# A decoder trunk with mixture-of-experts layers: expert matmuls in a fixed order, longer runs of expert weights, and one adaLN form for all tiles

## The chip, the cores and the metric

The kernel runs on one core of a Trainium2 chip. The metric is the device time of one launch in microseconds (us). A core has TensorE (PE, matrix multiplies; its loads of the stationary operand are shown apart as PEld), VectorE (DVE), ScalarE (ACT), GpSimd (POOL) and SyncE (SP, which here only issues transfers). Sixteen DMA engines move data between HBM and the core's SBUF; matmuls accumulate in PSUM.

## The reference

Two layers on 512 tokens of width 1024, float32. Each has a token mixer (layer 0: sparse attention; layer 1: HGRN2, a gated linear recurrence) and then a mixture of experts. Every sub-layer has an RMS norm, and an adaLN shift, scale and gate made from one conditioning vector `c`.

```python
cond = silu(c)
for layer in range(2):
    mod = einsum('bd,sde->sbe', cond, ada_w[layer]) + ada_b[layer][:, None, :]   # s: mixer, experts
    shift, scale, gate = split(mod[0], 3, axis=-1)
    h = rms_norm(x, norm_g[layer, 0]) * (1.0 + scale[:, None, :]) + shift[:, None, :]
    y = nsa_mixer(h, ...) if layer == 0 else hgrn2_mixer(h, ...)
    x = x + gate[:, None, :] * y
    shift, scale, gate = split(mod[1], 3, axis=-1)
    h = rms_norm(x, norm_g[layer, 1]) * (1.0 + scale[:, None, :]) + shift[:, None, :]
    # experts: top group of 4, then the top 2 of its 4 experts for each token; 16 experts in all
    #   expert(t) = (silu(t @ w1[e]) * (t @ w3[e])) @ w2[e],  w1, w3: 1024 x 512, w2: 512 x 1024
    y = hier_moe(h, ...)
    x = x + gate[:, None, :] * y
```

`ada_w` is 2 x 2 x 1024 x 3072; the kernel treats it as 24 tiles of 1024 x 512, 6 for each of the four sub-layers.

## The kernel before

The stages follow each other: mixer of layer 0 (to about 420 us), its output product and the routing (to 500), its experts (to 775), mixer of layer 1 (to 1105), its output product and the routing (to 1180), its experts (to 1450), and the last sums. In the trace's names: `w` is a 2 MB tile of any weights, `hg` gathered token rows, `hgt` their transpose, `h_ps` the hidden products, `g` the gated hidden rows, `gT` their transpose, `y_ps` the output products, `yd` the results' rows in HBM, `xnd` the normalised token rows in HBM, `ada_ps` an adaLN product, `Q`, `K`, `Tc` the level operands of the recurrence.

*Experts* (`Moe.experts`). Sixteen positions p, fullest expert first; position p takes at most `CAPS[p]` rows: 96 three times, 128 once, 96 six times, 64 six times. A row block of 64 (or 32) rows is the stationary operand, and 2 (or 4) matmuls that write different column groups of PE run side by side: `BLOCKS` cuts 96 into 64 + 32 and 128 into 64 + 64. For each expert:
- `gather` (L1416, POOL): the rows from `xnd`.
- `transposed` (L1428 on PE; the shift and scale are applied as the transposes leave PSUM, on ACT and DVE).
- `hidden` (L1452): w1 and w3 against the transposed rows, in two halves of the 1024 inputs; then silu on ACT (L1456) and the product with the w3 side on DVE (L1458).
- `hidden_T` (L1465): four transposes of the gated rows, left by ACT as `gT`.
- `store` (L1479): w2; the adaLN gate on DVE (L1482); the rows go to `yd`.

The program's order inside one step i is gather and weights of expert i + 4, `hidden_T` of i, `transposed` of i + 2, `store` of i, `hidden` of i + 1. The framework's scheduler may reorder independent instructions on an engine by its own cost estimates; the four calls on PE are independent enough to be interleaved.

Each expert's weights are three 2 MB tiles: the first halves of w1 and w3 (part 0), the second halves (part 1), and w2 (part 2). Nine buffers hold three experts' tiles, and the next load waits for the one that it replaces. Nearly all loads are issued on SP, in the order part 0, 1, 2 (`load_part`: L1196 for w1 and w3, L1200 for w2). Input row k * 128 + p lies in partition p as block k, so w1 and w3 arrive in runs of 2 KB (one row of 512 float32) and w2 in runs of 4 KB.

*adaLN* (`ada_parts`). Tiles 0 to 15 are made by matmuls (L185): the conditioning column is the stationary operand, four column groups side by side, in four steps of eight matmuls (each float32 matmul is two instructions). Tiles 16 to 23 (the gate of layer 1's mixer, and all six of its experts) are made otherwise: ACT scales the eight row blocks by the conditioning value (L192), POOL adds them up in three additions (L198), and four matmuls with a column of ones finish the sum (L202). These eight tiles are worked on between the steps of layer 1's mixer (`merge(heads(), ada, HADA)` in `hgrn_heads`); they share the ring of two weight buffers with that mixer's own weights.

*Layer 1's mixer* (`hgrn_heads`, `hgrn_levels`). For each of eight heads, nine levels: DVE multiplies Q (L1080) and K (L1081) by running products, PE multiplies them in small blocks (L1043, L1057, L1063, L1068, L1073). In between PE works on the input product (`pr_ps`, L337 to L343), which the program advances beside the heads.

*Before the experts* (`mix_out`, `prepare`, `tokens`). Output product, new x, RMS norm of the token rows (`rms_rows`, L251 to L255), which are stored to `xnd` from ACT; the router's logits come from a separate transpose (L1226 writes them).

## Time and profile before

| | us |
|---|---|
| median of 3 runs (lowest, highest) | 1475.61 (1474.67, 1477.06) |
| the profiled execution | 1478.35 |
| its span, first to last instruction | 1476.5 |

| engine | busy us | share of the span |
|---|---|---|
| PE | 1291.1 | 87% |
| PEld | 767.6 | 52% |
| DVE | 723.1 | 49% |
| ACT | 468.1 | 32% |
| POOL | 225.5 | 15% |

HBM is read for 320.73 MB in all. A row of the profile names line, engine, operation, what is written and read by the kernel's names, and shapes; in rows in order of time the first two numbers are start and length in us, and the bracket holds the idle time of the engine before the instruction and what ended it. "issue" means that nothing the profile shows was waited for. Rows that begin with a:b give for a stretch of the span its length, then the busy time of PE, PEld, DVE, ACT and POOL (with counts), PE's granted clock (1.00 is full speed), the mean busy share of the 16 DMA engines and GB/s; an engine that did nothing there is left out.

### The profile page before, as it was taken

To read this page: it belongs to the slowest core of one execution; us is meant where nothing else is said; L and a number is where in the kernel's file an instruction comes from. 1 tells how busy PE (TensorE), PEld (TensorE's weight loads), DVE (VectorE), ACT (ScalarE), POOL (GpSimd) and SP (SyncE) were. 2 spreads that over 40 slices of the span, in tenths; PEclk is the share of its full clock that TensorE was granted. 3 is DMA by queue.
4 is the path that set the end of the run, shared out by engine and by line. 5 is a ranking of instruction groups with operands and counts; after the bars stand their busy time and mean duration, and the time that the engine had idled before them with its cause. 6 is when DMAs were issued, how large, how long until landed. Compare 5 with 4: busy or idle time off the path is not lost. (4 is left out here: it accounts for less than half of the span.)

```text
span 1476.5 us, 25266 instructions
## 1 busy us (share of the span) xinstructions
PE 1291.1 (87%) x10122; PEld 767.6 (52%) x10123; DVE 723.1 (49%) x1791; ACT 468.1 (32%) x1071; POOL 225.5 (15%) x198
## 2 busy tenths in 40 slices
PE   4998899988989699999983998888979699999983
PEld 3776555765558333333323866566767543333330
DVE  2636886468854722222217476777665641222213
ACT  2523555336533211111115434344533121111110
POOL 1202212222100100000014025222130100000002
PEclk9999999999999799999996999999989799999997
DMA  9702552634564899999986222433338699999995
GB/s 354 206 11 85 176 185 91 252 121 152 192 265 157 282 368 343 376 381 334 384 325 182 86 103 87 157 115 115 115 115 299 235 343 365 360 377 335 367 397 193
DMA packets 168733, 346.42 MB, mean 235 GB/s; under 512 B 17236, under 2 KB 40620, under 8 KB 168605
## 3 DMA queue, kind: packets, MB, share of 16 engines
q1 hardware_dynamic: 135984, 276.80, 52.6%
q0 software_dynamic: 10560, 38.54, 8.0%
q10 hardware_dynamic: 22060, 29.34, 6.0%
q8 instruction: 84, 1.38, 0.4%
q14 instruction: 45, 0.36, 0.1%
HBM read 320.73 MB, written 23.93 MB: 233 GB/s over the span
## 5 line engine op out<-in xcount | busy, mean ns | idle before, releaser
L1452 PE MATMUL h_ps<-w,hgt 128*32 128x256 f32 (+1 forms) x2240 | 332.9, 488 | 0.0
L1452 PEld LDWEIGHTS h_ps<-w,hgt 128*32 128x32 f32 (+1 forms) x2240 | 111.8, 123 | 203.1 <-issue 172.4
L1479 PE MATMUL y_ps<-w,gT 128*32 128x256 f32 (+1 forms) x1120 | 163.6, 499 | 2.5 <-ACT gT L1468 2.1
L1458 DVE TENSOR_TENSOR g<-h_ps,g 32x256 f32<-32x256 f32 (+1 forms) x70 | 38.9, 556 | 253.7 <-ACT g L1456 253.1
L1456 ACT ACTIVATE g<-h_ps 64x512 f32<-64x512 f32 (+1 forms) x52 | 26.8, 516 | 368.2 <-PE h_ps L1452 346.2
L337 PE MATMUL pr_ps<-whi,hThi 128*128 128x512 f32 x288 | 119.6, 417 | 1.8 <-DVE qn L498 1.8
L338 PE MATMUL pr_ps<-wlo,hThi 128*128 128x512 f32 x288 | 115.6, 401 | 0.3 <-DVE wlo L311 0.3
L339 PE MATMUL pr_ps<-whi,hTlo 128*128 128x512 f32 x288 | 115.7, 402 | 0.2 <-DVE hTlo L283 0.2
L1479 PEld LDWEIGHTS y_ps<-w,gT 128*32 128x32 f32 (+1 forms) x1120 | 54.9, 125 | 97.3 <-issue 81.3
L1482 DVE TENSOR_TENSOR y<-y_ps,gate 128x512 f32<-128x512 f32 (+1 forms) x52 | 31.1, 598 | 123.3 <-PE y_ps L1479 107.5
L311 DVE TENSOR_TENSOR wlo<-w,whi 128x512 fp32r<-128x512 f32 x120 | 79.7, 702 | 23.0 <-ACT whi L310 22.8
L310 ACT ACTIVATE whi<-w 128x512 fp32r<-128x512 f32 x120 | 70.8, 629 | 39.0 <-SPq L1589 14.2
L782 ACT ACTIVATE P<-P,nm 128x128 f32<-128x128 f32 (+3 forms) x128 | 70.9, 556 | 36.9 <-DVE nm L780 35.8
L1416 POOL DMA_INDIRECT hg<-xnd,gidxp x26 | 23.7, 913 | 384.8 <-PE hg_tp L1428 383.0
L776 PE MATMUL s_ps<-kT,qT 128*128 128x256 f32 (+3 forms) x256 | 64.8, 358 | 12.0 <-DVE qn L498 6.9
L198 POOL TENSOR_TENSOR w<-w 128x2048 f32<-128x2048 f32 (+2 forms) x24 | 67.0, 2792 | 47.3 <-ACT w L192 46.1
L780 DVE CUSTOM_DVE_ANT_0 P<-s_ps,tb 128x128 f32<-128x128 f32 (+3 forms) x128 | 59.5, 485 | 21.5 <-PE s_ps L776 18.8
L1436 DVE TENSOR_SCALAR hgt<-hg_tp,mod 128x96 f32<-128x96 f32 (+2 forms) x128 | 43.7, 365 | 41.9 <-PE hg_tp L1428 36.4
L337 PEld LDWEIGHTS pr_ps<-whi,hThi 128*128 128x128 f32 x288 | 55.6, 193 | 15.1 <-issue 3.3
L339 PEld LDWEIGHTS pr_ps<-whi,hTlo 128*128 128x128 f32 x288 | 55.4, 192 | 12.2 <-DVE hTlo L283 0.4
L338 PEld LDWEIGHTS pr_ps<-wlo,hThi 128*128 128x128 f32 x288 | 55.9, 194 | 11.0 <-DVE wlo L311 0.7
L821 PE MATMUL p_tp<-ident,P 128*128 128x128 f32 x320 | 52.8, 282 | 8.2 <-DVE P L796 7.9
(361 smaller groups left out, 2121.9 us busy)
## 6 DMA issues: line engine op xcount, KB each, us to landing
w<-in_moe_w_dram SPq DMA_DIRECT2D x120, 1024.0 KB, 9.7
w<-in_moe_w_dram SPq DMA_DIRECT2D x32, 2048.0 KB, 9.5
w<-in_ada_w_dram SPq DMA_DIRECT2D x22, 2048.0 KB, 9.3
w<-in_hgrn_w_in_dram SPq DMA_DIRECT2D x12, 1024.0 KB, 6.9
tb<-tabd ACTq DMA_DIRECT2D x16, 456.0 KB, 3.8
yd<-y ACTq DMA_DIRECT2D x56, 128.0 KB, 5.0
w<-in_nsa_w_in_dram SPq DMA_DIRECT2D x3, 2048.0 KB, 8.1
yd<-zero POOLq DMA_DIRECT2D x12, 512.0 KB, 9.6
```

The lines of the kernel that those rows point to most:

```text
L198: nc.gpsimd.tensor_tensor(w[:, 0:n], w[:, 0:n], w[:, n:2 * n], op=ALU.add)
L310: nc.scalar.activation(a, w[:, k], AF.Copy)
L311: nc.vector.tensor_sub(b, w[:, k], a.bitcast(F32))
L337: nc.tensor.matmul(ps, hi[:, k, c], a, start=(k == 0), stop=False)
L338: nc.tensor.matmul(ps, hi[:, k, c], b, start=False, stop=False)
L339: nc.tensor.matmul(ps, lo[:, k, c], a, start=False, stop=(k == NK - 1))
L776: nc.tensor.matmul(sp[:, :n], qT[:, (hd + j) % 8, 128 * t:128 * t + 128], kT[:, v, br, gl, :n], start=(v == 0), stop=(v == 1))
L780: nc.vector.tensor_tensor_reduce(ps, sp[:, :n], tbs[hd + j][:, 384 - 128 * t:512], scale=-1.0, scalar=3.0e38, op0=ALU.add, op1=ALU.min, ac ...
L782: nc.scalar.activation(ps, ps, AF.Exp, bias=nm[:, i:i + 1], scale=-1.0, accum_out=z[:, i:i + 1])
L821: nc.tensor.transpose(tp[:, 128 * (t - kc):128 * (t - kc) + 128], Ps[j][:, offs[t] + 128 * kc:offs[t] + 128 * kc + 128], ident)
L1452: nc.tensor.matmul(ps[m * j:m * j + m, :w], hgt[:, k, r:r + m], ws[half][:, x + i, c:c + w], start=(k == 0), stop=(k == NK - 1))
L1479: nc.tensor.matmul(ps[m * j:m * j + m, :w], gT[:, f, r:r + m], w2v[:, f, w * j:w * j + w], start=(f == 0), stop=(f == 3))
```

## The change

- *Experts' order.* Every PE instruction of the experts gets an ordering edge to the one before it (`pe`), so that PE runs them in the program's order. `hidden` becomes a generator, and one step's order is: half 0 of the first row block of expert i + 1; transposes of the gated rows of i; transposes of the gathered rows of i + 2; half 0 of the second block (or half 1, where there is one block); `store` of i, second block first; half 1 of i + 1; then the gating.
- *Expert weights.* Partition p takes input rows 4 p to 4 p + 3 of a half (of w2: rows 4 p to 4 p + 3), which are one run of 8 KB (16 KB) in HBM. The token rows' columns are permuted to match, in two strided instructions as they are normalised (`spread`); the shift and scale columns are permuted by 16 small matmuls a layer (`modp`, in `prepare`); the gated rows are written to a new tile `go` with a stride.
- *adaLN.* All 24 tiles are made by matmuls; ACT's scaling and POOL's additions of tiles 16 to 23 go.

```diff
         def part(t, w):
-            if 6 * (2 * l + s) + t < POOLED:
-                ps = mm_ps("ada_ps")
...
-            else:
-                for k in range(NK):
-                    nc.scalar.activation(w[:, k], w[:, k], AF.Copy, scale=cond[:, k:k + 1])
...
-                    nc.gpsimd.tensor_tensor(w[:, 0:n], w[:, 0:n], w[:, n:2 * n], op=ALU.add)
...
+            ps = mm_ps("ada_ps")
+            for q in range(0, NK, 2):
+                side_by_side([lambda k=k, g=g: nc.tensor.matmul(
+                    ps[32 * g:32 * g + 32, 0:128], cond[:, k:k + 1].to_broadcast([128, 32]),
+                    w[:, k, 128 * g:128 * g + 128], start=(k == 0), stop=(k == NK - 1))
+                    for k in (q, q + 1) for g in range(4)])
                 yield
...
+    def spread(a):
+        return a.rearrange("q (h p i) -> q h i p", h=2, i=4)
...
-        nc.vector.tensor_scalar(dst, src, rs, None, op0=ALU.mult)
+        if order:
+            for half in range(2):
+                nc.vector.tensor_scalar(dst.rearrange("q (h i p) -> q h i p", h=2, i=4)[:, half], order(src)[:, half],
+                                        rs, None, op0=ALU.mult)
+        else:
+            nc.vector.tensor_scalar(dst, src, rs, None, op0=ALU.mult)
...
+            pp = tp_ps("mp_ps")
+            for i in range(4):
+                for g in range(4):
+                    nc.tensor.matmul(pp[32 * g:32 * g + 32, 4 * i:4 * i + 4], ident[:, i::4], self.mod[:, g::4],
+                                     start=True, stop=True)
+            self.modp = self.pool.tile([128, 16], F32, name="modp")
...
-                    eng.dma_start(out=w[:, 4 * i:4 * i + 4],
+                    eng.dma_start(out=w[:, 4 * i:4 * i + 4].rearrange("p k n -> p (k n)"),
                                   in_=I[name][self.l, e, 512 * part:512 * part + 512]
-                                  .rearrange("o (k p) n -> p (o k) n", p=128))
+                                  .rearrange("o (p k) n -> p (o k n)", p=128))
             else:
...
-                              in_=I["moe_w2"][self.l, e].rearrange("o (f p) n -> p (o f) n", p=128))
+                              in_=I["moe_w2"][self.l, e].rearrange("o (p f) n -> p (o f n)", p=128))
...
+        def pe(self, ins):
+            if self.in_order:
+                if self.last is not None:
+                    edge(ins, self.last)
+                self.last = ins
...
+            n = len(blocks)
+            product(0, 0)
+            yield
+            for b in range(1, n):
+                product(0, b)
+            if n == 1:
+                product(1, 0)
+            yield
+            if n > 1:
+                for b in range(n):
+                    product(1, b)
...
-                    nc.vector.tensor_mul(gt[r:r + m, w * j:w * j + w], ps[64 + m * j:64 + m * j + m, :w],
-                                         gt[r + m * j:r + m * j + m, :w])
-            return gt
+                    nc.vector.tensor_mul(go[r:r + m].rearrange("q (f p) -> q p f", f=4)[:, 2 * m * j:2 * m * j + 2 * m],
+                                         ps[64 + m * j:64 + m * j + m, :w].rearrange("q (p f) -> q p f", f=4),
+                                         gt[r + m * j:r + m * j + m, :w].rearrange("q (p f) -> q p f", f=4))
+            yield go
...
-            for r, m in blocks:
+            for r, m in reversed(blocks):
...
             def steps(i):
                 step("hg", i + 4, lambda p: self.gather(self.slot_tokens(p), CAPS[p]))
                 step("w", i + 4, self.weights)
+                step("h", i + 1, lambda p: self.hidden(S.pop(("hgt", p)), S["w", p], BLOCKS[CAPS[p]]))
+                h = S.pop(("h", i + 1), None)
+                if h:
+                    next(h)
                 step("gT", i, lambda p: self.hidden_T(S.pop(("g", p)), CAPS[p]))
                 step("hgt", i + 2, lambda p: self.transposed(S.pop(("hg", p)), CAPS[p]))
+                if h:
+                    next(h)
                 step("y", i, lambda p: self.store(S.pop(("gT", p)), S.pop(("w", p))[2],
...
-                step("g", i + 1, lambda p: self.hidden(S.pop(("hgt", p)), S["w", p], BLOCKS[CAPS[p]]))
+                if h:
+                    S["g", i + 1] = next(h)
```

More of the change, by code (lines that the diff above doesn't have):

```diff
@@ L181, in part @@
         def part(t, w):
-            if 6 * (2 * l + s) + t < POOLED:
-                ps = mm_ps("ada_ps")
-                for q in range(0, NK, 2):
-                    side_by_side([lambda k=k, g=g: nc.tensor.matmul(
-                        ps[32 * g:32 * g + 32, 0:128], cond[:, k:k + 1].to_broadcast([128, 32]),
-                        w[:, k, 128 * g:128 * g + 128], start=(k == 0), stop=(k == NK - 1))
-                        for k in (q, q + 1) for g in range(4)])
-                    yield
-            else:
-                for k in range(NK):
-                    nc.scalar.activation(w[:, k], w[:, k], AF.Copy, scale=cond[:, k:k + 1])
-                    if k % 2:
-                        yield
-                n = NK
-                while n > ADDED:
-                    n //= 2
-                    nc.gpsimd.tensor_tensor(w[:, 0:n], w[:, 0:n], w[:, n:2 * n], op=ALU.add)
-                ps = mm_ps("ada_ps")
-                for k in range(n):
-                    for g in range(4):
-                        nc.tensor.matmul(ps[32 * g:32 * g + 32, 0:128], onef.to_broadcast([128, 32]),
-                                         w[:, k, 128 * g:128 * g + 128], start=(k == 0), stop=(k == n - 1))
+            ps = mm_ps("ada_ps")
[4 more added lines that the diff above has]
+                    for k in (q, q + 1) for g in range(4)])
                 yield
@@ L247, with rms_rows @@
     normed = []
-    def rms_rows(dst, src, n):
+    def spread(a):
+        return a.rearrange("q (h p i) -> q h i p", h=2, i=4)
+    def rms_rows(dst, src, n, order=None):
         ss = small.tile([128, 1], F32, tag="ss", name="ss")
@@ L1156, in __init__ @@
             self.loads = [(part, p) for p in range(16) for part in range(3)]
+            self.in_order, self.last = False, None
         def begin(self, eng):
@@ L1427, in transposed @@
                     k = 4 * j + i
-                    nc.tensor.transpose(tp[:, rows * i:rows * i + rows], hg[0:rows, 128 * k:128 * k + 128],
-                                        ident[0:rows, 0:rows])
+                    self.pe(nc.tensor.transpose(tp[:, rows * i:rows * i + rows], hg[0:rows, 128 * k:128 * k + 128],
+                                                ident[0:rows, 0:rows]))
                 for i in range(4):
@@ L1443, in hidden, with product @@
             gt = pool.tile([128, 512], F32, tag="g", bufs=1, name="g")
+            go = pool.tile([128, 512], F32, tag="go", bufs=1, name="go")
             pss = [mm_ps("h_ps") for _ in blocks]
-            for half in range(2):
-                for (r, m), ps in zip(blocks, pss):
-                    w = 8 * m
-                    cols = [(x, c) for x in (0, 4) for c in range(0, 512, w)]
-                    for i in range(4):
-                        k = 4 * half + i
-                        for j, (x, c) in enumerate(cols):
-                            nc.tensor.matmul(ps[m * j:m * j + m, :w], hgt[:, k, r:r + m], ws[half][:, x + i, c:c + w],
-                                             start=(k == 0), stop=(k == NK - 1))
+            def product(half, b):
+                (r, m), ps = blocks[b], pss[b]
+                w = 8 * m
+                cols = [(x, c) for x in (0, 4) for c in range(0, 512, w)]
+                for i in range(4):
+                    k = 4 * half + i
+                    for j, (x, c) in enumerate(cols):
+                        self.pe(nc.tensor.matmul(ps[m * j:m * j + m, :w], hgt[:, k, r:r + m], ws[half][:, x + i, c:c + w],
+                                                 start=(k == 0), stop=(k == NK - 1)))
+            n = len(blocks)
[9 more added lines that the diff above has]
+                    product(1, b)
             for (r, m), ps in zip(blocks, pss):
@@ L1464, in hidden_T @@
             for f in range(4):
-                nc.tensor.transpose(tp[:, rows * f:rows * f + rows], gt[0:rows, 128 * f:128 * f + 128],
-                                    ident[0:rows, 0:rows])
+                self.pe(nc.tensor.transpose(tp[:, rows * f:rows * f + rows], gt[0:rows, 128 * f:128 * f + 128],
+                                            ident[0:rows, 0:rows]))
             gT = self.outs.tile([128, 4, 128], F32, tag="gT", bufs=1, name="gT")
@@ L1478, in store @@
                     for j in range(128 // m):
[L1479 to L1480 removed]
+                        self.pe(nc.tensor.matmul(ps[m * j:m * j + m, :w], gT[:, f, r:r + m],
+                                                 w2v[:, f, w * j:w * j + w], start=(f == 0), stop=(f == 3)))
                 y = self.outs.tile([128, 512], F32, tag="y", bufs=2, name="y")[:, :w]
@@ L1496, in experts @@
             S = {}
+            self.in_order = True
             def step(name, p, f):
```

18 lines of the change are left out of this document (9 added, 9 removed).

## The prediction

> **What bounds the kernel now.** I read the engines' busy time by stretches of the span first, then PE's weight loads in order of time inside one expert, then the DMA queues of short windows, then PE's waits in the second mixer. (The chain that ended last breaks off at the final row gathers and tells nothing here.) The profiled execution took 1478.35 us, 2.7 us above the median of 1475.61; sums below are made against it.
>
> ```profile
> span 1476.5 us, 25266 instructions
> ```
>
> The stretches, with PE's busy time, its granted clock, the DMA engines' share and rate in the last columns: the two expert stages, the end of the first, the 36 us in it with the fullest DMA, and the middle of the second mixer.
>
> ```profile
> 499.00:772.00 273.00, 264.28 (x1868) 100.09 (x1870) 64.27 (x188) 46.10 (x107) 17.55 (x20) 0.98 0.99 357
> 1180.00:1449.00 269.00, 260.63 (x1860) 98.91 (x1862) 63.87 (x184) 46.12 (x107) 17.09 (x19) 0.98 1.00 357
> 700.00:772.00 72.00, 64.86 (x316) 22.72 (x314) 12.56 (x27) 11.43 (x28) 4.65 (x5) 0.95 0.98 362
> 720.00:756.00 36.00, 32.03 (x154) 11.07 (x150) 6.62 (x14) 5.71 (x14) 0.00 (x0) 0.94 1.04 397
> 855.00:1085.00 230.00, 202.23 (x2304) 154.92 (x2303) 161.76 (x301) 99.17 (x192) 74.43 (x31) 0.94 0.32 105
> ```
>
> In both expert stages PE is busy for 97% of the time and the DMA engines are full too: two limits lie almost on each other, and a change there has to lift both. In the second mixer PE is busy for 202 of 230 us, so some 28 us are idle, at a clock of 0.94.
>
> **The change part by part. 1, the order of the experts' matmuls.** One cycle of a 96-row expert, PE's weight loads in order of time (128*64 are matmuls for the 64-row block, two side by side; 128*32 those for the 32-row block, four side by side):
>
> ```profile
> 616.17 0.20 PEld L1479 LDWEIGHTS y_ps<-w,gT 128*64 128x64 f32 x4 [0.17 <-ACT gT L1468]
> ...
> 619.75 1.45 PEld L1479 LDWEIGHTS y_ps<-w,gT 128*32 128x32 f32 x32 [0.81 <-issue]
> 621.61 0.20 PEld L1452 LDWEIGHTS h_ps<-w,hgt 128*64 128x64 f32 x4 [0.41 <-issue]
> ...
> 624.33 1.45 PEld L1452 LDWEIGHTS h_ps<-w,hgt 128*32 128x32 f32 x32 [0.81 <-issue]
> 626.20 0.20 PEld L1452 LDWEIGHTS h_ps<-w,hgt 128*64 128x64 f32 x4 [0.41 <-DMA yd<-y]
> ...
> 628.40 0.14 PEld L1452 LDWEIGHTS h_ps<-w,hgt 128*64 128x64 f32 x2 [0.28 <-issue]
> 628.83 0.14 PEld L1452 LDWEIGHTS h_ps<-w,hgt 128*64 128x64 f32 x2 [0.29 <-issue]
> 629.78 1.45 PEld L1452 LDWEIGHTS h_ps<-w,hgt 128*32 128x32 f32 x32 [0.81 <-issue]
> 631.65 0.20 PEld L1452 LDWEIGHTS h_ps<-w,hgt 128*64 128x64 f32 x4 [0.41 <-DVE g L1458]
> ...
> 633.51 0.37 PEld L1465 LDWEIGHTS g_tp<-ident,g 96*128 96x128 f32 x4 [0.81 <-DVE g L1458]
> ```
>
> The starts give the price of each run. A whole half of a 64-row block takes 3.58 us (626.20 to 629.78). The other half is broken: its first part lies before the transposes (631.65 to 633.51, 1.86 us) and its rest after y (621.61 to 624.33, 2.72 us), together 4.58 us, so the break costs 1.00 us: a pair is split and each half runs alone for the pitch of a pair, 0.43 us (628.40 to 628.83), twice, and one more run ends. What a run's end costs: 3.58 less 8 x 0.43 is 0.14 us. After the change the order is: 64-row half 0 of the next expert, transposes, 32-row half 0 together with y's 32-row block, y's 64-row block together with 64-row half 1, 32-row half 1. Nothing is split, and two joints vanish: 1.00 + 2 x 0.14 = 1.28 us a cycle. The gating that the split run covered until now is covered by the whole half 0, 3.58 us instead of 1.86; were that cover too short, PE would wait in front of the transposes for it, and everything on PE behind that, since the order is now a chain.
>
> A 64-row expert:
>
> ```profile
> 719.85 7.04 PE L1452 MATMUL h_ps<-w,hgt 128*64 128x512 f32 x32
> 727.43 0.46 PE L1465 MATMUL g_tp<-ident,g 64*128 64x64 f32 x4 [0.55 <-DVE g L1458]
> ```
>
> Here PE waits 0.55 us for the gating before each transpose. With y and the next half 0 in between the wait goes, and a joint of 0.14: 0.7 us. Per stage: nine 96-row experts 11.5 us, six 64-row ones 4.2, the 128-row one, which has the wait and the joint, 0.7; less 2 us because the first has none before it and the last none behind it. The clock of 0.95 in the last 72 us is 3.6 us lost behind these waits; I count 2.6 of it. That makes 17 us per stage if the weights arrive.
>
> The strided write of the gated rows (go) and the stride in their reading lengthen three DVE multiplies a cycle; I cost it at nothing, since half 0 hides it; in the last expert nothing does, under 1 us.
>
> **2, the weights in 8 and 16 KB runs.** The same bytes in a quarter of the packets. Two short windows of the DMA queues price a packet: 570 to 575 us, where w1 and w3 in 2 KB runs are alone, and 564 to 567 us with w2 in 4 KB runs on this queue (packets, MB, share of 16 engines):
>
> ```profile
> q1 hardware_dynamic: 830, 1.70, 93.9%
> ```
> ```profile
> q1 hardware_dynamic: 277, 1.03, 85.6%
> ```
>
> 0.939 x 80 us / 830 = 90.5 ns for 2048 B; 0.856 x 48 / 277 = 148 ns for 3.72 KB on average. The line through both is 20 ns and 34.4 ns per 1000 B: 161 ns for 4096 B, 302 for 8192, 584 for 16384. An expert costs 2048 x 90.5 + 512 x 161 ns = 268 us of engine time, over 16 engines 16.7 us; afterwards 512 x 302 + 128 x 584 = 229 us, or 14.3 us. The other end is no gain at all, packets in proportion to bytes: 16.7 us. I take 15.3, nearer to the line, because its two points already show the step. The Trainium skill (DMA: Bandwidth & Descriptors, Specifications) puts the line rate at transfers of 512 B and more; by that rule 2 KB is as good as 8 KB and the sum is the 16.7. The step from 22.6 to 25.1 B/ns between the two windows speaks against it.
>
> Is that enough? 357 GB/s over 273 us are 97.5 MB. Ended 17 us sooner, they need 381 GB/s on average; 397 is what the fullest 36 us show with the old packets. The slack now, from the issue of the last w2, the median from issue to landing of w2 between 720 and 756 us (last number), and the last expert's y:
>
> ```profile
> 744.44 2.42 SPq L1200 DMA_DIRECT2D w<-in_moe_w_dram  x1
> ```
> ```profile
> w<-in_moe_w_dram SPq DMA_DIRECT2D x2, 2048.0 KB, 16.9
> ```
> ```profile
> 769.60 3.65 PE L1479 MATMUL y_ps<-w,gT 128*64 128x512 f32 x16 [0.53 <-ACT gT L1468]
> ```
>
> The last w2 lands near 761 and is used at 769.6, 8 us on. PE 17 us sooner eats those 8 and needs 9 more; 1.4 us for each of the 13 experts loaded in the stage are 18. So the weights keep up, not by much. Buffers come free in another order (half 0's 5 us before w2's instead of after it), which bunches issues on SP but leaves the number the same; the three experts of prefetch cover it. Two stages: 34 us.
>
> **3, the second mixer's adaLN.** Eight tiles lose eight ACT scalings, three POOL additions and eight matmul instructions each, and get 64 matmul instructions. What the additions do besides being busy:
>
> ```profile
> 894.39 8.47 POOL L198 TENSOR_TENSOR w<-w 128x2048 f32<-128x2048 f32 x3 [6.64 <-ACT w L192]
> ```
> ```profile
> L1081 DVE TENSOR_TENSOR K<-K,Tc x56: 409/418/4759, 852.9 to 1097.5; 128x256 f32<-128x256 f32 x56
> ```
> ```profile
> PE lvB_ps L1043 <- DVE K L1081: 6.9, 2, 6.2
> PE lvC_ps L1063 <- DVE K L1081: 6.7, 2, 3.5
> PE lvC_ps L1068 <- DVE K L1081: 4.8, 2, 3.4
> PE lvB_ps L1057 <- DVE K L1081: 4.3, 1, 4.3
> PE lvA_ps L1043 <- DVE K L1081: 3.6, 2, 2.0
> ```
>
> DVE's K multiply takes 0.42 us, but up to 4.76 where it meets a POOL addition on SBUF, and PE then stands idle for K: 26.3 us between 855 and 1085. Nearly all of it lies under the additions; I count 24. Behind each gap the clock falls: 0.06 of 230 us are 13.8 us, a quarter of it while PE is idle anyway, so 10. Gain 34. The price: sixteen matmul instructions of this form hold PE from 223.43 to 224.00, 0.57 us, while the old form's eight took 0.36:
>
> ```profile
> 223.43 0.64 PE L185 MATMUL ada_ps<-w,cond 128*32 128x128 f32 x16
> 224.00 0.44 PE L821 MATMUL p_tp<-ident,P 128*128 128x128 f32 x2
> ```
> ```profile
> 1057.38 0.43 PE L202 MATMUL ada_ps<-w,onef 128*32 128x128 f32 x8
> 1057.74 0.50 PE L337 MATMUL pr_ps<-whi,hThi 128*128 128x512 f32 x1
> ```
>
> 8 x (4 x 0.57 - 0.36) = 15.4 us on a PE that is the bound where nothing disturbs it. Net 34 - 15.4 = 18.6; I take 16, because DVE's level chain will keep some gaps. With 4 steps a tile in place of 5 the tiles finish earlier, their two ring buffers are held for shorter, and SP's loads of the mixer's weights behind them come no later.
>
> **4, small parts.** The permuted mod columns are 16 tiny matmuls (32 instructions) a layer. Nothing in the trace has their shape; at best they hide in PE's gaps for nothing, at worst they hold PE twice as long as the 16 instructions above, 1.1 us. I take half of that: two layers, +1 us. The token rows' normalisation becomes two DVE instructions with a stride in place of one. Behind the last of them DVE waits 0.96 us for the last logits anyway, which hides a few tenths:
>
> ```profile
> 1166.50 0.24 DVE L1226 SCALAR_TENSOR_TENSOR logits<-lg_ps,rs,brow 128x20 f32<-128x20 f32 x1 [0.96 <-PE lg_ps L1225]
> ```
>
> Sum: 1478.35 - 34 - 16 + 1 = 1429.4; less the 2.7 of this execution, 1427.
>
> **The rivals.** *A: packets do not get cheaper, and DMA becomes the bound of the expert stages.* For it: share 0.99 already. The 17 us of PE meet 8 us of slack, so 8 per stage remain: 1476 - 16 - 16 + 1 = 1445. *B: the mixer gains nothing*, because PE's 15.4 us arrive in full and DVE's level chain, not POOL, sets the gaps: 1476 - 34 + 1 = 1443. Against it: a median of 0.418 us and a maximum of 4.759 for one shape. *C: the expert stages gain nothing*, HBM being at its limit: 97.5 MB at the stage's 357 GB/s are the 273 us it takes now; 1476 - 16 + 1 = 1461. The 397 GB/s of 36 us speak against it. The Trainium skill (DMA: Bandwidth & Descriptors, Where 436 GB/s comes from) has HBM bind at about 358 GB/s per core, which is this rival; by that rule, the 397 should not be there. *D, slower: long packets are slow.* The instruction queue's packets are 16 KB:
>
> ```profile
> q8 instruction: 84, 1.38, 0.4%
> ```
>
> 0.004 x 16 x 1476.5 / 84 = 1.12 us each. With that for w2 alone an expert takes 128 x 1.12 / 16 = 9.0 us for w2 and 11.6 for the rest; with 2.2 us of gathers and result rows (0.8 MB at the 22.6 B/ns above) that is 22.8 us, for 13 experts 296 us: from 499 to 795, and y 3.7 us behind it, 799 in place of 772. That is +27 a stage: 1476 + 54 - 16 + 1 = 1515. It decides from about 21 us an expert on, where 13 of them fill the 273 us of now. Those packets come from one other queue, one at a time, which makes it unlikely.
>
> **How the numbers follow.** Forecast 0.55 (1412 to 1440), A 0.17, B 0.13, C 0.08, D 0.07. No change is within 0.2%, 3 us, about what a measurement of this kernel can tell. All but D are faster; I give "same" 0.03, split off C, and "slower" 0.09 for D and what I do not see. The range 1408 to 1464 takes in A, B and C and leaves out D and a little below.
>
> **What would show it.** Right: runs of 16 and 64 matmul instructions in PE's order and cycles near 17.2 us for 96-row experts; mixer additions gone, K at 0.42 us throughout, no half clock between 860 and 1080; q1 with a quarter of the packets at 8 KB near 300 ns. Wrong: PE waiting for weights from the thirteenth expert on (A), for the gating before the transposes, or q1's time per byte higher than now (D).

## The result and the profile after

The changed kernel takes 1452.36 us (median of 4 runs, 1450.10 to 1454.64) against 1475.70 us for the kernel before in the same session (4 runs, 1474.67 to 1477.06): a ratio of 0.9841, 95% interval 0.9824 to 0.9859, or 23.3 us less. The forecast was 48.7 us less (1427). The profiled execution took 1451.84 us.

Divided at the same places of the program, the two profiled executions compare like this (the experts of layer 0 begin with the first transpose of gathered rows, the expert stages end with their last output product, the change-over lies between that and the mixer's first input product, the mixer ends at its first output product; e1 to e15 are the experiments below):

| us | to experts | experts 0 | change-over | mixer 1 | product, routing | experts 1 | end |
|---|---|---|---|---|---|---|---|
| before | 500.0 | 273.2 | 26.6 | 298.5 | 82.3 | 272.6 | 23.3 |
| after | 502.2 | 256.8 | 30.9 | 287.3 | 84.4 | 257.8 | 30.4 |
| e1 adaLN alone | 500.2 | 273.0 | 26.5 | 281.4 | 83.8 | 273.3 | 23.1 |
| e2 long runs alone | 504.2 | 274.7 | 26.6 | 303.3 | 84.1 | 272.0 | 23.4 |
| e3 order alone | 500.0 | 263.7 | 31.3 | 301.5 | 82.4 | 263.9 | 30.4 |
| e4 order and long runs | 501.9 | 258.2 | 31.4 | 299.0 | 82.6 | 258.9 | 30.6 |
| e5 expert 14 earlier | 501.9 | 257.8 | 27.8 | 287.5 | 84.5 | 259.4 | 23.7 |
| e8 fewer loads | 502.1 | 248.7 | 30.0 | 285.4 | 84.8 | 250.3 | 30.1 |
| e9 shift | 500.8 | 255.7 | 32.7 | 282.7 | 84.6 | 259.6 | 31.2 |
| e15 both repairs | 500.7 | 258.0 | 29.5 | 282.8 | 84.2 | 261.1 | 22.9 |

So the expert stages gave 31.2 us, close to the 34 forecast, but the two places behind them took 11.4 back; the mixer gave 11.2 where 16 were forecast. The rows of the table differ by 26.7 us and the medians by 23.3, since before's profiled execution lies 2.7 us above its median and after's 0.5 below. The profiled executions of e2 (6.1 us above its median), e5, e8 and e15 (3.3 to 3.8 below) lie further off, so a difference of a few us over a whole row of these says little. Three of these stretches of before, in the stretch view (columns as before):

```profile
773.20:799.80 26.60, 2.84 (x16) 2.56 (x14) 18.91 (x34) 11.00 (x20) 8.51 (x9) 0.54 0.51 140
799.80:1098.30 298.50, 263.27 (x2815) 203.33 (x2813) 207.55 (x396) 128.80 (x249) 84.81 (x42) 0.93 0.36 120
1453.20:1476.50 23.30, 0.02 (x2) 0.00 (x0) 10.60 (x9) 0.00 (x0) 3.74 (x4) 0.60 0.57 193
```

and the same with the expert stages, of after:

```profile
502.20:759.00 256.80, 253.01 (x1872) 99.23 (x1872) 73.27 (x182) 46.02 (x107) 12.51 (x15) 0.99 0.98 374
759.00:789.90 30.90, 2.87 (x14) 2.57 (x14) 19.13 (x34) 11.01 (x20) 12.22 (x13) 0.56 0.56 176
789.90:1077.20 287.30, 270.63 (x3259) 209.00 (x3257) 174.24 (x395) 93.38 (x188) 17.61 (x18) 0.97 0.37 126
1161.60:1419.40 257.80, 253.52 (x1872) 100.78 (x1872) 73.18 (x181) 46.05 (x107) 12.06 (x14) 0.99 0.96 367
1419.40:1449.80 30.40, 0.04 (x2) 0.00 (x0) 10.92 (x9) 0.00 (x0) 7.52 (x8) 0.59 0.62 217
```

In the mixer PE's idle time fell from 35.2 us to 16.7 and POOL's work from 84.8 to 17.6; PE's own busy time rose by 7.4. In the expert stages PE is busy for 98.5 and 98.3% and the DMA engines still have next to no free share (0.98, 0.96).

The cycle of a 96-row expert, PE's weight loads in order of time, is as foretold: unbroken runs, and a pitch (the time from one expert's transposes to the next one's) of 17.19 us (520.43 to 537.62) where before had 18.48 (first after, then the two transposes of before):

```profile
520.43 0.37 PEld L1488 LDWEIGHTS g_tp<-ident,go 96*128 96x128 f32 x4 [0.81 <-issue]
...
521.57 1.45 PEld L1462 LDWEIGHTS h_ps<-w,hgt 128*32 128x32 f32 x32
523.11 1.64 PEld L1502 LDWEIGHTS y_ps<-w,gT 128*32 128x32 f32 x32
525.16 0.20 PEld L1502 LDWEIGHTS y_ps<-w,gT 128*64 128x64 f32 x4 [0.41 <-issue]
...
532.17 1.45 PEld L1462 LDWEIGHTS h_ps<-w,hgt 128*32 128x32 f32 x32 [0.81 <-issue]
534.04 0.20 PEld L1462 LDWEIGHTS h_ps<-w,hgt 128*64 128x64 f32 x4 [0.41 <-issue]
...
537.62 0.37 PEld L1488 LDWEIGHTS g_tp<-ident,go 96*128 96x128 f32 x4 [0.81 <-issue]
```
```profile
517.96 0.37 PEld L1465 LDWEIGHTS g_tp<-ident,g 96*128 96x128 f32 x4 [0.81 <-DVE g L1458]
...
536.44 0.36 PEld L1465 LDWEIGHTS g_tp<-ident,g 96*128 96x128 f32 x4 [0.81 <-DVE g L1458]
```

The end is where the new loss is plainest. `ys` are gathered rows of `yd` that experts up to 14 wrote, `yk` are the rows that may come from expert 15; both are weighted and added to x on DVE. DVE and POOL at the end of before:

```profile
1438.78 0.69 DVE L1482 TENSOR_TENSOR y<-y_ps,gate 128x512 f32<-128x512 f32 x1 [4.75 <-PE y_ps L1479]
1443.31 0.95 POOL L1661 DMA_INDIRECT ys<-yd,cr  x1 [57.87 <-DMA yd<-y]
1453.27 0.69 DVE L1482 TENSOR_TENSOR y<-y_ps,gate 128x512 f32<-128x512 f32 x1 [6.31 <-PE y_ps L1479]
1453.88 4.86 DVE L1665 SCALAR_TENSOR_TENSOR x<-ys,cw,x 128x1024 f32<-128x1024 f32 x4
1459.61 0.93 POOL L1661 DMA_INDIRECT yk<-yd,cr  x1 [11.62 <-DVEq L1589]
```

and of after:

```profile
1414.90 0.69 DVE L1505 TENSOR_TENSOR y<-y_ps,gate 128x512 f32<-128x512 f32 x1 [1.75 <-PE y_ps L1502]
1419.48 0.69 DVE L1505 TENSOR_TENSOR y<-y_ps,gate 128x512 f32<-128x512 f32 x1 [3.89 <-PE y_ps L1502]
1421.15 0.95 POOL L1694 DMA_INDIRECT ys<-yd,cr  x1 [65.83 <-PEq L1622]
1426.37 5.35 DVE L1698 SCALAR_TENSOR_TENSOR x<-ys,cw,x 128x1024 f32<-128x1024 f32 x4 [6.19 <-DMA ys<-yd,cr]
1433.39 0.94 POOL L1694 DMA_INDIRECT yk<-yd,cr  x1 [7.56 <-issue]
```

Before, expert 14's rows were ready 14.5 us ahead of expert 15's (1438.78, 1453.27), so the first gathers and the way there lay under expert 15's products and the additions began at once. After, the lead is 4.6 us: the second half of expert 15's hidden product stands ahead of expert 14's output product in the fixed order. The first gathers come behind everything, the additions wait 6.2 us for them, and the last gathers start 13.9 us behind the last product's gate instead of 6.3.

### The profile page after: what moved, and what is told of

Its sections match the earlier page's. It is cut to its first block, busy times and chain, and to the rows that moved or that the text cites. A ratio compares the mean times of both kernels' runs of the same rounds, so it can differ in the third digit from the quotient of the medians.

```text
span 1449.8 us, 26218 instructions
## 1 busy us (share of the span) xinstructions
PE 1274.5 (88%) x10634; PEld 771.6 (53%) x10635; DVE 715.1 (49%) x1801; ACT 429.7 (30%) x1007; POOL 157.0 (11%) x174
## 5 line engine op out<-in xcount | busy, mean ns | idle before, releaser
L1462 PE MATMUL h_ps<-w,hgt 128*32 128x256 f32 (+1 forms) x2240 | 324.8, 490 | 6.9 <-DMA w<-in_moe_w_dram 6.9
L1502 PE MATMUL y_ps<-w,gT 128*64 128x512 f32 (+1 forms) x1120 | 159.1, 485 | 1.1 <-ACT gT L1491 1.1
L1480 DVE TENSOR_TENSOR go<-h_ps,g 32x256 f32<-32x256 f32 (+1 forms) x70 | 58.8, 840 | 133.9 <-ACT g L1478 133.7
L1502 PEld LDWEIGHTS y_ps<-w,gT 128*64 128x64 f32 (+1 forms) x1120 | 57.0, 123 | 88.8 <-issue 75.0
L1505 DVE TENSOR_TENSOR y<-y_ps,gate 128x512 f32<-128x512 f32 (+1 forms) x52 | 31.2, 599 | 136.7 <-PE y_ps L1502 131.8
L302 DVE TENSOR_TENSOR wlo<-w,whi 128x512 fp32r<-128x512 f32 x120 | 80.9, 706 | 23.1 <-ACT whi L301 19.9
L1444 DVE TENSOR_SCALAR hgt<-hg_tp,modp 128x96 f32<-128x96 f32 (+2 forms) x128 | 43.6, 366 | 97.5 <-PE hg_tp L1436 92.0
L182 PE MATMUL ada_ps<-w,cond 128*32 128x128 f32 x1536 | 64.0, 295 | 19.9 <-DMA w<-in_ada_w_dram 14.5
L1491 ACT ACTIVATE gT<-g_tp 128x384 f32<-128x384 f32 (+2 forms) x32 | 14.6, 458 | 164.2 <-PE g_tp L1488 146.9
L1424 POOL DMA_INDIRECT hg<-xnd,gidxp x26 | 23.7, 912 | 363.2 <-PE hg_tp L1436 360.4
L329 PEld LDWEIGHTS pr_ps<-wlo,hThi 128*128 128x128 f32 x288 | 55.3, 192 | 11.4 <-DVE wlo L302 0.6
## 6 DMA issues: line engine op xcount, KB each, us to landing
w<-in_moe_w_dram SPq DMA_DIRECT2D x32, 2048.0 KB, 11.4
```

The lines of the kernel that those rows point to most:

```text
L182: side_by_side([lambda k=k, g=g: nc.tensor.matmul(ps[32 * g:32 * g + 32, 0:128], cond[:, k:k + 1].to_broadcast([128, 32]), w[:, k, 128 * g ...
L302: nc.vector.tensor_sub(b, w[:, k], a.bitcast(F32))
L329: nc.tensor.matmul(ps, hi[:, k, c], b, start=False, stop=False)
L1462: self.pe(nc.tensor.matmul(ps[m * j:m * j + m, :w], hgt[:, k, r:r + m], ws[half][:, x + i, c:c + w], start=(k == 0), stop=(k == NK - 1)))
L1480: nc.vector.tensor_mul(go[r:r + m].rearrange("q (f p) -> q p f", f=4)[:, 2 * m * j:2 * m * j + 2 * m], ps[64 + m * j:64 + m * j + m, :w].r ...
L1502: self.pe(nc.tensor.matmul(ps[m * j:m * j + m, :w], gT[:, f, r:r + m], w2v[:, f, w * j:w * j + w], start=(f == 0), stop=(f == 3)))
```

## The experiments

Each ratio is to the kernel before in the same session, with its 95% interval.

**The parts alone.** e1, the adaLN hunk of the change on the kernel before:

```diff
-            if 6 * (2 * l + s) + t < POOLED:
...
+            ps = mm_ps("ada_ps")
+            for q in range(0, NK, 2):
+                side_by_side([lambda k=k, g=g: nc.tensor.matmul(
```

> The kernel before with one part of the change alone: all eight adaLN steps of the second mixer as matmuls on the raw weights. The forecast's third step: 24 us of TensorE's idle time under GpSimd's additions and 10 us of half clock go, 15.4 us of matmuls come, so 1475.7 - 16 = 1460 us. What the two traces show by stage (mixer -11.2 us, projection after it +2.5): 1466 to 1468 us, with TensorE now waiting for adaLN weights for about 6 us that it did not wait for before. The rival that the K waits only change their place: 1475 to 1477 us.

1459.91 us, ratio 0.9879 (0.9849 to 0.9909): 14.8 us less, where the forecast has 16. The 1466 to 1468 us that I had read from the stages of the two traces was wrong. Its mixer in the stretch view:

```profile
799.70:1081.10 281.40, 266.67 (x3259) 206.51 (x3257) 174.47 (x395) 93.78 (x188) 17.66 (x18) 0.99 0.39 128
```

Against before PE's idle time falls by 20.5 us (24 were forecast), and its busy time rises by 3.4 (forecast: 15.4 of new matmuls, less 10 for the clock). The same instructions in the same order take 5.9 us less here than in the changed kernel; e9 asks why.

e2, on the kernel before, the long runs with all that fits them (`load_part`, `spread`, `modp`, `go`):

```diff
-                                  .rearrange("o (k p) n -> p (o k) n", p=128))
+                                  .rearrange("o (p k) n -> p (o k n)", p=128))
```

> The kernel before with one part of the change alone: expert weights in 8 and 16 KB runs, with the token rows, the adaLN columns and the gated rows permuted to fit; the experts' matmuls are left to the old order and the second mixer's adaLN is the old one. The forecast costs this at +1 us for the permuted adaLN columns and nothing for the strided gating multiply: 1474 to 1478 us. The rival that the weights' transfers bind the expert stages of before: 10 us or more faster (under 1466 us). The rival that the strided multiply (0.84 us on the mean against 0.56) is on TensorE's path without the fixed order to cover it: 0.3 to 0.5 us for each of 32 experts, 1485 to 1492 us.

1484.21 us, ratio 1.0058 (1.0039 to 1.0077): close to the last case in time. Yet its expert stages are 1.5 us longer and 0.6 us shorter than before's; 4.8 us lie in the mixer of layer 1, where each engine's instructions stand as before, and 4.2 ahead of the experts, where `spread` and `modp` are new. The profiled execution was also the slowest of nine. So the strided multiply was not shown to be the cause, and e14 tries it again.

e3, on the kernel before, the order alone:

```diff
+            self.in_order = True
...
+                step("h", i + 1, lambda p: self.hidden(S.pop(("hgt", p)), S["w", p], BLOCKS[CAPS[p]]))
```

> The kernel before with one part of the change alone: the experts' matmuls in the fixed order of unbroken runs; the weights still come in 2 and 4 KB runs and the adaLN is the old one. If the order itself gives the gain and the transfers keep up: 34 us in the two stages less about 11 us at their ends, 1452 us. If the long runs are needed for it (16.7 us of transfers for an expert of 2 and 4 KB runs against a cycle of 17.2 and, in the 64-row experts, 11.3 us): the stages end at the transfers' pace and the gain is 12 to 16 us less the same 11 us, 1470 to 1475 us.

1472.43 us, ratio 0.9978 (0.9962 to 0.9994): the second case. The stages gain 9.5 and 8.7 us and lose 11.8 behind them.

e4, the changed kernel with the old adaLN:

```diff
+            if 6 * (2 * l + s) + t < POOLED:
...
+            else:
+                for k in range(NK):
+                    nc.scalar.activation(w[:, k], w[:, k], AF.Copy, scale=cond[:, k:k + 1])
```

> The changed kernel with the old adaLN of the second mixer: the fixed order and the long runs together. By the traces' stages the experts give -31.2 us, the change-over behind the first expert stage +4.3 and the end +7.1, early drift +2: 1458 us. By the forecast, which has nothing at the two ends: 1475.7 - 33 = 1443 us. With e1 it shows if the two halves of the change add up to the whole (-23.3 us).

1464.53 us, ratio 0.9911 (0.9881 to 0.9940): slower than I expected by 6.5 us. Its two stages give 28.7 of the 31.2 us, and part of the rest is that the expectation was read against before's profiled execution, 2.7 us above its median. Its mixer, 299.0 us, is still the old one. Long runs add 5.5 and 5.0 us to the order's gain in the stages, though alone they gave nothing there. The parts do not simply add: in the new order the last 64-row experts wait for their weights, and the long runs ease that (in layer 0 two of their pitches are 18.0 and 17.1 us in e3, 15.7 and 15.4 in e4).

**The ends of the expert stages.** e5, on the changed kernel:

```diff
-                if h:
+                if h and i != 14:
                     next(h)
                 step("y", i, lambda p: self.store(S.pop(("gT", p)), S.pop(("w", p))[2],
...
+                if h and i == 14:
+                    next(h)
```

> The changed kernel with the second product of expert 14 ahead of the second half of expert 15's hidden product instead of behind it. Theory (the fixed order moved expert 14's output to 4.6 us before the last one, where it was 13.3 us, and the gathers of the earlier experts' rows, the additions and then the last gathers wait for it): expert 14's rows are stored 2.7 us earlier, the last product comes 3 us later since its gating is no longer covered, the last gathers start 3 to 4 us earlier; 6 to 8 us less over both layers, 1445 us. Rival (the 7.1 us at the end come from something else, such as the clock): the last product's 3 us are lost twice, 1456 to 1458 us.

1448.35 us, ratio 0.9813 (0.9796 to 0.9831), 4 us under the changed kernel. In the profile, which is its fastest execution, the end is back to 23.7 us and the change-over to 27.8; the stages pay 1.0 and 1.6 (DVE and POOL of e5 in order of time):

```profile
1409.13 0.69 DVE L1505 TENSOR_TENSOR y<-y_ps,gate 128x512 f32<-128x512 f32 x1 [10.35 <-DMA w<-in_moe_w_dram]
1413.65 0.95 POOL L1696 DMA_INDIRECT ys<-yd,cr  x1 [59.95 <-DMA yd<-y]
1418.96 0.69 DVE L1505 TENSOR_TENSOR y<-y_ps,gate 128x512 f32<-128x512 f32 x1 [4.75 <-PE y_ps L1502]
1419.57 4.87 DVE L1700 SCALAR_TENSOR_TENSOR x<-ys,cw,x 128x1024 f32<-128x1024 f32 x4
1426.06 0.94 POOL L1696 DMA_INDIRECT yk<-yd,cr  x1 [7.73 <-issue]
```

The rows of expert 14 are 9.8 us ahead again, and the last gathers start 7.1 us behind the last product's gate instead of 13.9. Of the 7.1 us at the end 6.7 come back, of the change-over's 4.3 come 3.1, and that shows their cause. The timed gain is less sure than the cause: the medians differ by 4.0 us, and the two intervals overlap a little.

e6, the changed kernel without the branch for tokens over capacity:

```diff
-            m.overflow()
+            pass
```

> The changed kernel without the branch behind each expert stage that treats tokens over an expert's capacity (with these inputs no token is over it; the comparison, the jump and what every engine does at the two sides of it are left out). Theory: the last gathers (first at 1433.39 us) wait at the branch until the first gathers have landed (1430.5 us) and the additions on VectorE are done; without it they are issued behind the first ones at about 1426 us: 7 us less at the end and 5 to 7 behind the first stage, 1438 to 1440 us. Rival (the last gathers wait for the memory that the additions free, not for the branch): 1 to 2 us less at each place, 1449 to 1451 us.

1443.72 us, ratio 0.9780 (0.9759 to 0.9800). Half of each theory. At the end the branch is what the last gathers wait for: without it the first `yk` starts at 1426.37 us, while DVE still adds `ys` (to 1431.60), and the end takes 22.0 us instead of 30.4. With the branch the first `yk` starts only when the last of these additions is done: 1.7 us behind it in after (1431.72, 1433.39), 1.6 in e5 (1424.44, 1426.06) and 0.9 in before (1458.74, 1459.61), by the rows above. Behind the first stage nothing is gained (31.2 us): there `yk` waits for DVE's addition of `ys` without the branch too, as the last row shows (POOL and DVE of e6 in order of time, at the end and behind the first stage).

```profile
1424.05 0.93 POOL L1694 DMA_INDIRECT ys<-yd,cr  x1 [0.30 <-issue]
1426.37 0.94 POOL L1694 DMA_INDIRECT yk<-yd,cr  x1 [1.39 <-DMA yd<-y]
1427.75 3.85 DVE L1698 SCALAR_TENSOR_TENSOR x<-ys,cw,x 128x1024 f32<-128x1024 f32 x3 [1.45 <-DMA ys<-yd,cr]
```
```profile
771.51 3.55 POOL L1694 DMA_INDIRECT yk<-yd,cr  x1 [7.58 <-DVE x L1698]
```

**The strided multiply.** e7, the changed kernel with

```diff
-                    nc.vector.tensor_mul(go[r:r + m].rearrange("q (f p) -> q p f", f=4)[:, 2 * m * j:2 * m * j + 2 * m],
...
+                    nc.vector.tensor_mul(go[r:r + m, w * j:w * j + w], ps[64 + m * j:64 + m * j + m, :w],
```

> The changed kernel with the gating multiply written in plain column order instead of every fourth column; its columns then meet other rows of the second weight, so the hidden units are paired wrongly; all else is as in the changed kernel. If the longer strided multiply (0.84 us mean against 0.56) is covered by the fixed order, as the forecast had it, but for the last expert: 0 to 1 us less, 1451 to 1452 us. If it is on the way of each expert: 0.3 us and more for each of 32, 1442 us or less.

1454.04 us, ratio 0.9853 (0.9833 to 0.9874): no gain, although DVE's multiply is a third shorter (groups by line, first after, then e7). Half 0 covers it, as the prediction had it.

```profile
L1480 DVE TENSOR_TENSOR go<-h_ps,g 32x256 f32<-32x256 f32 (+1 forms) x70 | 58.8, 840 | 133.9 <-ACT g L1478 133.7
```
```profile
L1480 DVE TENSOR_TENSOR go<-h_ps,g 32x256 f32<-32x256 f32 (+1 forms) x70 | 38.9, 555 | 143.9 <-ACT g L1478 143.4
```

e14, the same edit on e2's kernel:

> The kernel of e2 (long runs alone, old order) with the gating multiply in plain column order; hidden units are paired wrongly with the second weight's rows. e2 was 9.5 us slower than before though its expert stages were not (274.7 and 272.0 us against 273.2 and 272.6). If the strided multiply is what costs, because the old order does not cover it: 1470 to 1476 us. If e2's loss comes from elsewhere (its mixers, whose instructions stand in the same order as before, took 2 and 5 us more): 1482 to 1487 us.

1480.97 us, ratio 1.0036 (1.0016 to 1.0056): between the two cases and nearer to the second. Why the long runs alone make the old order slower stays open.

**The weights.** e8, the changed kernel with, in `weights`:

```diff
+            if e in (11, 13):
+                for _ in range(3):
+                    self.loads.pop(0)
+                self.loaded += self.loaded[-3:]
+                return self.loaded[-3:]
```

> The changed kernel with the weights of the experts at places 11 and 13 not loaded (those of the places 10 and 12 are used again), so 12 MB less are read in each layer; the products are the same in number. Theory: the last 64-row experts are bound by the weights (pitches 13.7 to 16.7 and 15.4 to 13.8 us where TensorE alone needs 11.3): both come down to 11.3 to 11.5 us, 6 to 8 us less in each layer, 1437 to 1440 us. Rival (those pitches are long for another reason, the order at the end or the clock): 1450 to 1453 us.

1436.50 us, ratio 0.9740 (0.9719 to 0.9761), 15.9 us under the changed kernel, and the stages are 8.1 and 7.5 us shorter. PE in order of time on the last 64-row experts of layer 0, second halves of `hidden`, first after, then e8:

```profile
724.59 1.02 PE L1462 MATMUL h_ps<-w,hgt 128*64 128x512 f32 x2
726.91 3.65 PE L1462 MATMUL h_ps<-w,hgt 128*64 128x512 f32 x14 [1.30 <-DMA w<-in_moe_w_dram]
...
739.94 1.04 PE L1462 MATMUL h_ps<-w,hgt 128*64 128x512 f32 x2 [0.55 <-DMA w<-in_moe_w_dram]
742.34 3.65 PE L1462 MATMUL h_ps<-w,hgt 128*64 128x512 f32 x14 [1.36 <-DMA w<-in_moe_w_dram]
```
```profile
723.87 3.60 PE L1462 MATMUL h_ps<-w,hgt 128*64 128x512 f32 x16
```

The pitches of these experts come down to 11.3 us, as the theory has it. So the weights do bind at the end of the changed kernel, by 8 us a stage. e10 tried to give that back by the order of the experts:

```diff
-CAPS = [96] * 3 + [128] + [96] * 6 + [64] * 6
+CAPS = [96] * 3 + [128, 96, 64, 96, 64, 96, 64, 96, 64, 96, 96, 64, 64]
```

> The changed kernel with the 64-row experts placed between the 96-row ones (96 x3, 128, 96, 64, 96, 64, 96, 64, 96, 64, 96, 96, 64, 64) instead of all six at the end; the same work and the same bytes. Theory (an expert's weights take about 14.4 us, more than the 11.3 us of a 64-row expert and less than the 17.2 us of a 96-row one, and the buffers hold three experts): with the short ones spread the weights are ahead everywhere, every pitch is TensorE's own, each expert stage 6 to 8 us shorter, 1437 to 1440 us. Rival (a short expert behind a long one waits for its weights wherever it stands, since loads are issued as buffers come free): the waits are spread as well, 1449 to 1453 us.

1457.43 us, ratio 0.9874 (0.9857 to 0.9891), 5 us slower than after; its stages are 260.0 and 257.8 us. The theory fell (layer 0): the alternating part ran at pitches of 13.6 and 15.2 us, but the last long experts then came out at 15.5 to 18.7. Two windows of after's DMA queues correct its 14.4 us an expert, 600 to 660 us and 720 to 752 us (packets, MB, share of 16 engines):

```profile
q1 hardware_dynamic: 2323, 20.07, 87.2%
q10 hardware_dynamic: 1329, 1.45, 6.9%
q0 software_dynamic: 352, 1.18, 6.6%
```
```profile
q1 hardware_dynamic: 1816, 13.03, 97.4%
```

While 96-row experts run, the rows stored to `yd` (q10) and gathered (q0) take 13.5% of the same engines. Weights come at 20.07 MB in 60 us, 18.8 us for an expert's 6.29 MB, against a pitch of 17.2: PE eats the lead there already. Longer runs bought nothing there, for the same 60 us of before, among 96-row experts too, have nearly as many bytes in 3.6 times the packets:

```profile
q1 hardware_dynamic: 8479, 19.98, 90.5%
```

Nearly alone, at the end, the weights come at 15.4 us an expert (13.03 MB in 32 us), and 15.4 us is also the time from expert 13's transposes to expert 14's (730.5 to 745.9). That fits e10, in that a transfer without free time anywhere gains nothing from another order of the experts; no run isolates it.

e11, both edits (e5's and e10's), and e12, e11 with e9's edit:

> Both of the last: the 64-row experts spread as in e10, and expert 14's second product ahead of the second half of expert 15's hidden product as in e5. If their gains (4 us by the times of e5, 14 by the theory for e10) add up: 1433 to 1436 us. If the order at the end only matters while the weights are late: as e10.

> The kernel of e11 with the 64 more transposes of e9. By the theory of e9 its second mixer has the length of e9's and not of e11's, 3 to 6 us less than e11, about 1430 us; by its rival as e11 or 1 us more.

1456.29 us (0.9867, 0.9850 to 0.9884) and 1454.43 us (0.9860, 0.9842 to 0.9878). On the spread order e5's edit gives next to nothing, but not because of the order at the end: PE has expert 14's product as early as in e5, and DVE, whose order nothing fixes, takes expert 15's gating multiply ahead of its gate. Expert 14's lead comes to 4.7 us (6.1 at the end). So these two runs don't tell whether the edits would add up (PE and DVE of e11 in order of time, behind the first stage; e5's DVE has the gate at 749.90 and the gating at 753.96):

```profile
745.67 3.65 PE L1502 MATMUL y_ps<-w,gT 128*64 128x512 f32 x16 [0.53 <-ACT gT L1491]
753.43 1.03 DVE L1480 TENSOR_TENSOR go<-h_ps,g 64x512 f32<-64x512 f32 x1 [12.35 <-ACT g L1478]
754.49 0.69 DVE L1505 TENSOR_TENSOR y<-y_ps,gate 128x512 f32<-128x512 f32 x1
759.21 0.69 DVE L1505 TENSOR_TENSOR y<-y_ps,gate 128x512 f32<-128x512 f32 x1 [4.03 <-PE y_ps L1502]
```

The mixer is 288.2 us in e11 and 282.6 in e12, which bears out e9 (below).

e13, as e8 at the places 5 and 7 (`if e in (5, 7):`):

> As e8, but the weights not loaded are those of the places 5 and 7, in the middle of the 96-row experts, whose pitch is TensorE's own 17.2 us in the changed kernel; the same 12 MB less in each layer. If the weights already fall behind while the 96-row experts run (with the gathers and the row stores on the same 16 engines a middle fifth of the stage moves weights at some 337 GB/s, 18.7 us for an expert's 6.3 MB): the lead saved there is still there at the end, both expert stages come to e8's length, 1435 to 1438 us. If the lead is full when the 64-row experts begin and these are only too quick for it: the last pitches stay at 13.7 to 16.7 and 15.4 us, 1450 to 1453 us.

1472.66 us, ratio 0.9974 (0.9960 to 0.9987): neither case, and no answer to its question. The tiles used twice are held for two experts, loads on SP wait for them in order (none is issued from 602 to 634 us), and the stages take 268.2 and 267.0 us with 12 MB less. The lead lost in mid-stage was not made up.

**The mixer's missing 6 us.** Two gaps of PE in the changed kernel's mixer have no releaser (nothing that the profile shows ended them: "issue"). The larger one in PE's order of time, and the instruction queue in a window of 1.3 us from 1032.4 on:

```profile
1031.24 0.41 PE L182 MATMUL ada_ps<-w,cond 128*32 128x128 f32 x4 [0.48 <-DMA w<-in_ada_w_dram]
1034.96 1.07 PE L182 MATMUL ada_ps<-w,cond 128*32 128x128 f32 x12 [3.31 <-issue]
```
```profile
q8 instruction: 1, 0.02, 5.3%
```

One 16 KB packet starts there, at 1032.50, and PE goes on 2.5 us later; for the other gap (848.4 to 850.05) one starts at 847.48, 2.6 us ahead. The same holds in every run: the mixers of all kernels with the new adaLN have 19 gaps of over 0.5 us without a releaser, and each ends 2.3 to 2.6 us behind the start of a 16 KB packet; those with the old adaLN have none. Full DMA engines are not what these two gaps share: from 1032.4 us on the mixer's weights fill them to 98.7%, from 847.4 on they carry next to nothing but the packet. Between two such packets PE runs some 260 instructions on average in this mixer, but 550 between the last two packets ahead of the gap at 848.4 and 459 between those ahead of the larger one. Why these packets start so late stays open. e9 moves the places:

```diff
-        nc.tensor.transpose(tp[:, 0:16], lb16, ident[0:16, 0:16])
+        for _ in range(65):
+            nc.tensor.transpose(tp[:, 0:16], lb16, ident[0:16, 0:16])
```

> The changed kernel with one small transpose of the change-over between expert stage and second mixer issued 65 times instead of once, while TensorE has nothing else to do: 64 more weight loads and 64 more matmuls in its stream, so that every later place in the stream lies half a 16 KB instruction packet further on. Theory (two gaps inside an adaLN step, 1.66 and 3.31 us with no wait by the profile, end 2.3 to 2.6 us behind the start of a 16 KB packet of the instruction queue: TensorE has run out of instructions; where a packet ends decides if it happens): these gaps move or shrink, the second mixer's 287.3 us come down to 281 to 284, 3 to 6 us less in all, 1447 to 1449 us. Rival (the gaps belong to the adaLN step itself, whatever the place of the packets): gaps at the same matmul, mixer 287 us, 1452 to 1454 us.

1450.27 us, ratio 0.9844 (0.9822 to 0.9866). The mixer comes down to 282.7 us as the theory says, with one gap left, now inside the level products and 1.70 us long:

```profile
1029.49 0.23 PE L1035 MATMUL lvA_ps<-Q,K 128*32 128x32 f32 x3 [1.70 <-issue]
```

The timed gain is not outside the interval, and the change-over is 1.8 us longer by the added transposes. With e12 and e15 (282.6, 282.8 us) against the eight kernels with the new order and the new adaLN that lack the shift (285.4 to 289.5) the effect on the mixer is shown. Without PE's time of "issue" the mixers of these eleven, and of e1, are all 280 to 284 us.

e15, e5's and e9's edits together:

> Both edits that helped, on the changed kernel with its own order of experts: expert 14's second product earlier (e5) and the 64 more transposes (e9). If they add up: about 1446 us (4 us less by e5, 2 us less by e9), and under both 1448 and 1450 us. If the shift only moves the gaps of TensorE's stream elsewhere: 1448 to 1450 us.

1444.73 us (1441.11 to 1446.62, 5 runs), ratio 0.9793 (0.9772 to 0.9814): the best version with the whole computation, 7.6 us under the changed kernel, and the two repairs together give at least what they gave apart (e5 4.0, e9 2.1). Its interval lies below the changed kernel's.

## Why the prediction was wrong, by its own steps

- *Step 1, the order, 17 us per stage: the cycle was right, the sum close by luck*, 16.4 and 14.8 us. A 96-row expert gained 1.29 us where 1.28 was worked out (18.48 to 17.19), a 64-row one the 0.7 (12.06 to 11.35), half 0 is the cover, and the strided multiply costs nothing (e7). But two errors cancel in the sum. With the weights out of the way (e8) the stages are 24.5 and 22.3 us shorter than before's, not 17: from expert 13's transposes to the end of the last output product it takes 33.7 us in before and 23.3 in e8, in both stages, where the prediction took 2 us off for the edges. The late weights (step 2) then take 8.1 and 7.5 us back.
- *The step that failed is the sum of part 1: it ended at the last expert's y.* The order puts half 1 of expert i + 1 ahead of y of expert i; in the cycle that is free, but for the last pair y of 14 is what the row gathers wait for. It cost 4.3 + 7.1 us; e3 shows that with the order alone (4.7 and 7.1), and e5 undoes 3.1 and 6.7 of it. The prediction set the chain of waits aside because it breaks off at the final row gathers; it was the view that pointed at the place.
- *Step 2, the packets: right in price where the weights are nearly alone* (1816 packets at 97.4% of 32 us are 275 ns for 7.2 KB on the mean, 26.1 B/ns, where 2 KB had 22.6; 15.4 us an expert where 15.3 was taken), *wrong on "the weights keep up"*. The 15.3 us for an expert left out the gathers and row stores on the same engines, which were counted for rival D only. Beside them it is 18.8 us, and a packet costs more as well (20.07 MB at 87.2% of 60 us are 24.0 B/ns). Rival A's mechanism is there: PE waits for weights from the fourteenth expert on (724.59 above), and e8 prices it at 8 us a stage. By the rule of the Trainium skill (DMA: Bandwidth & Descriptors, Specifications) that transfers run at line rate from 512 B on, e4's stages should not be shorter than e3's. They are, by 5.5 and 5.0 us, so the measurement decides against it here.
- *Step 3, the mixer, 16 us: right alone* (e1, 14.8 us), *short in company*: 11.2 us in the mixer. The larger part of the difference is that PE ran out of instructions for 5.0 us, against 0.9 in e1 (PE's waits in the mixer, first after, then e1):

```profile
PE ada_ps L182 <- issue: 5.0, 2, 3.3
```
```profile
PE lvB_ps L1041 <- issue: 0.9, 1, 0.9
```

  That is a matter of where the 16 KB packets end. The prediction counted what 448 more matmul instructions cost in PE's time, not that they also have to be fetched. The clock fell with it: 0.97 in the mixer against 0.99 in e1 (before: 0.93).
- *Part 4, +1 us for modp, nothing for the strided normalisation*: not isolated. Of the +2.1 us in product and routing of layer 1, e1 shows 1.5 without them, and e4 only 0.3 with them. Ahead of layer 0's experts the three kernels without long runs stand at 500.0 to 500.2 us and all with them, and so with these parts, at 500.7 to 504.4; after has 2.2 us there.
- *The sum*: of the 25.4 us missed the ends are 11.4, the mixer 4.8, the expert stages 2.8, and the start with product and routing 3.3 beyond the 1 us forecast. The rest is that the profiled executions differ by more than the medians.
- *The rivals*: A came true in part; B, that the mixer gains nothing, and C, that the stages gain nothing, did not; nor did D. A change of both signs inside one part was not among them.

## What to carry to other kernels

When an order is fixed for the steady cycle, follow its last two rounds by hand up to whatever reads their results: what is overlap in the middle is delay at the end. Where two limits lie close together, cost the transfers with everything else that uses the same engines in that window, not the one queue that changes. An order fixed on one engine can be undone by another whose order is free (e11). And when instructions are added to a dense stretch, look for gaps without a releaser next to the instruction queue's packets.

## What the hardware showed that I had not expected

- PE stood without instructions for up to 3.3 us at a time in the changed kernel's mixer (5.5 in e6), and went on 2.3 to 2.6 us after the start of a 16 KB instruction packet. The Trainium skill (Runtime: NRT & Kernel Launch, Instruction fetch mechanics) has blocks of 16 KiB or 256 instructions, as the trace has, and calls the cost of crossing one mostly hidden; here it was not.
- A branch that is not taken cost 8.4 us (e6: 30.4 to 22.0 us at the end): POOL issued the gathers behind it only when DVE's additions ahead of it were done (0.9 to 1.7 us behind them in before, after and e5), and in after these additions wait for the first gathers.
- The same weights flowed at 334 GB/s beside gathers and row stores and at 407 GB/s nearly alone (20.07 MB in 60 us, 13.03 MB in 32 us). Beside them runs of 8 and 16 KB were no faster than runs of 2 and 4 KB (19.98 MB in 60 us of before).
